# Two transformer blocks on one core: seven small loads on another queue, three modulation steps earlier, and a rewritten entry to the second block

## The chip, the cores and the metric

The kernel runs on one core of a Trainium2 chip. The metric is the device time of one execution in microseconds (us); below, "the profiled execution" is a separate one that was recorded instruction by instruction. TensorE is the matrix engine, VectorE (DVE in the rows) and ScalarE (ACT) do elementwise work, GpSimd (POOL) and SyncE (SP) here mostly issue DMAs.

## The reference

A sequence of 256 tokens with 1024 features passes through two layers of a first block and one layer of a second one, all in float32. What matters here:

```
# first block, layer 0 (attention) and 1 (pooling), 6 modulation vectors per layer
m = silu(c) @ w_mod[i] + b_mod[i]            # 1024 -> 6 x 1024, one row
hx, hc = x*(1+sc1)+sh1, ctx*(1+csc1)+csh1
q, k, v = projections of hx and hc by w_qkv; q, k of hx rotated by cos/sin tables
y = differential attention(q, [k_ctx,k], [v_ctx,v], lam(attn_lambda)) -> rms * subln_g -> w_o
x = layer_norm(ALPHA*x + g1*y, ln_g, ln_b)
x = layer_norm(ALPHA*x + g2*(silu(h@Wg)*(h@Wu))@w_out, ln_g, ln_b)   # h = x*(1+sc2)+sh2
# second block
h = rms(x, norm1_g);  columns of h @ w_in: a_q a_k a_v i_q i_k i_w b_q b_kv b_g c_qkv gates
a: an index score (i_q, i_k, i_w) picks the top 64 keys per query, attention over these
b: compressed, selected and window attention;  c: dilated attention
x = x + (sum over a,b,c of sigmoid(gate) * branch) @ w_out;  then a gated FFN
```

## The kernel before, in words

Every large product is exact to float32 in three passes: an operand is split in a high part (rounded to the matmul's float32r format) and a low part (the rest), and `mm3` (lines 77 to 80) issues high by high, high by low and low by high. Weights come in units of 1 MB: `raw_load` (line 54) takes one of four "raw" buffers and loads it by SyncE; `wsplit` casts each half on ScalarE (line 70) and subtracts on VectorE (line 71) into one of two to four split slots. A raw buffer is free again when both halves are split, a split slot when its last product is done.

The framework orders each engine's instructions ahead of time, by program order and its own estimate of when each is ready; then each engine runs its list strictly in that order, waiting where an operand is missing. `behind(i)` forces the instructions in its scope that run on i's engine to stand after i on it. `mod_step` (line 210) gives its instructions a lower priority.

*Modulation.* Ten vectors of 1024 (called sh2, sc2, g1 and so on) are made by 80 small steps. A step loads 512 KB of `w_mod` by POOL into one of three `mraw` buffers (line 131) and accumulates it on VectorE (line 132). Steps are strung into other stages: 2 behind each of 16 attention scores, 3 behind each of the pairs 2 to 10 of the first FFN (`STEPS_IN`), 1 behind each of the 11 units of its output product (`STEPS_OUT`), then, at `mod_until("g1_1")`, what is left of the vector g1 of layer 1. The finished row is broadcast by TensorE (line 145), and the last products of the first FFN stand behind that (`mods["mm"]`). The same three buffers also hold the layer norms' rows.

*Attention's entry.* Inputs and weights come in four quarters (`load_quarter`, SyncE); after the fourth, `rest(3)` finishes the products of quarter 3. Then, behind the last modulate activation on ScalarE (`seq["mod"]`), ScalarE issues seven small loads: five into `prow` (norm gains and biases, which one TensorE transpose, line 648, turns into columns), `rope` (256 KB, cos and sin tables) and `lamr` (128 KB, the lambda vectors). `rope_T` (lines 676 to 691) multiplies the projections by the tables on VectorE (lines 684 to 687) and transposes them on TensorE (line 690) for the scores.

*An FFN* (`Ffn`): its first two pairs of weight units are multiplied token tile by token tile (`tile_products`), so that they can begin when the first tile is normed; the other nine in `rest`; `out` multiplies by the output weights, in which the last `held` units are kept for `finish(t, n)`, tile by tile.

*Entry of the second block.* The second FFN's `out` is followed, for each token tile t, by `pre` (add the residual), `layer_norm`, `rms` and `to_hT` (8 transposes on TensorE, line 320, scaling on ScalarE, line 333, split on VectorE, lines 336 and 337). Then the buffers of the first block are given back; KZ (the zero-padded keys) is cleared by POOL; `small` and `pr2` are loaded by POOL, and `pr2` (key gains and positions) is transposed (line 956). `project(512, 452)` makes PA (a_k, a_v, the index vectors); its first weight unit is split under the last products of the FFN, the second while tile 0 is normed. The index vectors are transposed and put into place (lines 1150 to 1161), then `normed_dup_T` norms a_k (`kn`), then come the index scores, the top 64 and `project(0, 512)` (the queries a_q). `gates(0)` follows the attention in program order but fills TensorE during it.

`keep_busy(n)` (line 98) issues n products of a tile of ones, whose result nobody reads.

Of the kernel before, what the change touches and what calls it, by code (L numbers as in the profile page):

```python
# [10 lines left out]
F32 = mybir.dt.float32  # L11
# [20 lines left out]
def tile_net(ctx: ExitStack, tc: tile.TileContext, I: dict, out: bass.AP):  # L32
# [315 lines left out]
    class Out:  # L348
# [7 lines left out]
        def part(self, u, wh, wl, t, n):  # L356
            mh, ml = self.mov
            tk = slice(t * 128, (t + 1) * 128)
            for k in range(2):
                kk = 2 * u + k  # L360
                mm3(self.P[t][n], mh[:, kk, tk], ml[:, kk, tk], wh[:, k, HALF[n]], wl[:, k, HALF[n]], kk == 0,
                    kk == 2 * self.nu - 1)
# [16 lines left out]
    class Ffn:  # L379
# [16 lines left out]

        def tile_products(self, t, hT):
            hh, hl = hT
            tk = slice(t * 128, (t + 1) * 128)
            for fp in range(self.FIRST):  # L400
# [69 lines left out]
    with tc.tile_pool(name="at", bufs=1, side="right", reuse_waits="tile") as at:  # L470
# [48 lines left out]
        def load_quarter(q):  # L519

            raws = [raw_load(wv0[:, :, j0 * 128:(j0 + 2) * 128], 8, 256) for j0 in (8 + 2 * q, 2 * q)]
            load_x("x", q)
            rw = wp.tile([128, 2048], F32, tag="raw", name="raw", bufs=4)
            rw = rw[:, :1536].rearrange("p (w k c) -> p w k c", w=3, k=2)
            for i, kind in enumerate((1, 0, 2)):
                sp.dma_start(rw[:, i], wq[:, 2 * q:2 * q + 2, kind * 1024:kind * 1024 + 256])
                if i == 1:
                    load_x("ctx", q)
            return raws, rw
# [41 lines left out]
        class Chunk:  # L571
# [19 lines left out]
            def products(self, ks, lat=True, con=True):  # L591
# [7 lines left out]
                if self.kind and con:  # L599
                    if self.PC is None:  # L600
                        self.PC = bank().rearrange("p (t c) -> p t c", t=2)
                    for t in range(2):
                        tk = slice(t * 128, (t + 1) * 128)
                        for k in ks:
                            if self.kind == 1:
                                mm3(self.PC[:, t, :], wh[:, k, tk], wl[:, k, tk], hc[0][:, k, :], hc[1][:, k, :],
                                    k == 0 and t == 0, k == 7, **kw)
                            else:
                                mm3(self.PC[:, t, :], hc[0][:, k, tk], hc[1][:, k, tk], wh[:, k, :], wl[:, k, :],
                                    k == 0 and t == 0, k == 7, **kw)  # L610

# [4 lines left out]
        def rest(q):  # L616
            ks = range(2 * q, 2 * q + 2)
            cv.products(ks, con=False)
            ck.products(ks, lat=False)

        for q in range(4):
            with behind(*((first_dma.ins,) if not q else ())):
                raws, rw = load_quarter(q)
            mod_quarter(q, raws)
            if not q:
# [12 lines left out]

        with behind(seq["mod"]):
            prow = cp.tile([128, 128], F32, name="prow")  # L640
            gp.memset(prow, 0.0)
            se.dma_start(prow[32:64], I["ln_g"].rearrange("l w (k c) -> (l w k) c", c=128))
            se.dma_start(prow[64:96], I["ln_b"].rearrange("l w (k c) -> (l w k) c", c=128))
            se.dma_start(prow[96:104], rows128(I["norm1_g_2"][0]))
            se.dma_start(prow[104:112], rows128(I["norm2_g_2"][0]))
            se.dma_start(prow[112:113], I["attn_subln_g"])
            pcol_ps = sbank()
# [6 lines left out]
            N1, N2 = pcol[:, 96:104], pcol[:, 104:112]  # L654
            rope = at.tile([128, 2, 2, 2, 64], F32, name="rope")
            se.dma_start(rope, I["k_rope"].rearrange("(t p) v w c -> p t v w c", p=128))
            lamr = at.tile([128, 256], F32, tag="aT", name="lamr", bufs=5)
            se.dma_start(lamr, I["attn_lambda"].rearrange("a b c -> a (b c)").to_broadcast([128, 256]))

# [230 lines left out]
    with tc.tile_pool(name="hid", bufs=1, side="right", reuse_waits="tile") as hidp:  # L890
# [17 lines left out]
        for t in range(2):  # L908
# [4 lines left out]
            n4.rms(t)  # L913
            n4.to_hT(t, hT, N1)
            if t == 0:
                with behind(n4.scaled[0]):
                    n4.pre(1, 1, o3.finish(1, 1), grow)

# [4 lines left out]
    blk1.close()  # L923
    wi = kview(I["w_in_2"][0])
# [3 lines left out]
    seq["w"] = 2  # L928
    extras.append(ctx.enter_context(tc.tile_pool(name="wz", bufs=1, side="right", reuse_waits="tile")))
    with tc.tile_pool(name="b2", bufs=1, reuse_waits="tile") as b2:  # L930

        KZ = b2.tile([128, 6, 2, 2, 256], F32R, name="KZ")
        for half in range(2):
            gp.memset(KZ[(1 - half) * 64:(2 - half) * 64, :, :, half, :].bitcast(F32), 0.0)

# [7 lines left out]
        small = b2.tile([128, 554], F32, name="small")  # L945
        gp.dma_start(small, I["k_small"])
        cmask, eo, bmask = small[:, 0:256], small[:, 256:384], small[:, 384:392]
        nmask = small[:, 392:426].rearrange("p (t n) -> p t n", t=2)
        sel32 = small[0:32, 426:554]
        pr2 = b2.tile([128, 128], F32, tag="t512", name="pr2", bufs=3)  # L950
        gp.memset(pr2, 0.0)
        gp.dma_start(pr2[0:32], I["nsa_cmp_pos_2"][0].rearrange("s (l a) d -> (s l) (a d)", a=2))
        for dup in range(2):
            gp.dma_start(pr2[32:38, dup * 64:(dup + 1) * 64], I["qk_norm_g_2"][0])
        b = tbank()
        pe.transpose(b[:, :128], pr2, ident)
        pc2 = b2.tile([128, 41], F32, name="pc2")
        ve.tensor_copy(pc2[:, 0:38], b[:, 0:38])
        ve.tensor_mul(pc2[:, 38:41], b[:, 32:38:2], pc2[:, 33:38:2])
        GA, GB, GC = pc2[:, 38:39], pc2[:, 39:40], pc2[:, 40:41]  # L960
# [45 lines left out]
        def put(hi, lo, src, scale):  # L1006

            se.activation(hi, src, AF.Copy, scale=scale)
            ve.scalar_tensor_tensor(lo, src, scale, hi.bitcast(F32), op0=ALU.mult, op1=ALU.subtract)

        def put_k(src, t, d0, scale=1.0):

            n, tk = src.shape[1], slice(t * 128, (t + 1) * 128)
            for half in range(2):
                p = slice(half * 64, (half + 1) * 64)
                put(KZ[p, d0:d0 + n, 0, half, tk], KZ[p, d0:d0 + n, 1, half, tk], src[p],
                    scale if isinstance(scale, float) else scale[p])

# [85 lines left out]

        def gates(br):
            g = b2.tile([128, 8, 256], F32, tag="gate", name="gate", bufs=1)
            for u in range(4):
                wh, wl = wunit(wi[:, :, 4572 + br * 1024 + u * 256:4572 + br * 1024 + (u + 1) * 256], 8, 256)
                G = bank().rearrange("p (a b) -> p a b", a=2)
# [35 lines left out]
        WA = [wtile(0, sp), wtile(4, sp)]  # L1145
        PA = project(512, 452)
        vA = b2.tile([128, 2, 64], F32, name="vA")
        iwc = b2.tile([128, 2, 4], F32, name="iwc")
        iqT = b2.tile([128, 2, 2, 256], F32R, tag="vv", name="iqT", bufs=1)
        for t in range(2):  # L1150
            se.copy(vA[:, t, :], PA[t][:, 64:128])
# [8 lines left out]
            put_q(iqT, bv[:, 0:2], t, 0)  # L1160
            put_k(bv[:, 2:3], t, 0)
        normed_dup_T(PA, 0, 1, 1, GA)
        madd = []
# [23 lines left out]
        for t in range(2):  # L1187
# [15 lines left out]
            split_oT(oA, 4, oTh, oTl, t)  # L1203
        gA_ = gates(0)
        P1 = project(1476, 384)
# [252 lines left out]
```

## Time and profile before

| | us |
|---|---|
| median of 3 runs | 1160.46 (1156.91, 1160.46, 1160.65) |
| the profiled execution | 1157.81 |
| its span, from first to last instruction | 1156.0 |
| TensorE busy in it | 1129.1 |
| VectorE busy | 829.0 |
| ScalarE busy | 575.8 |

[...] Times are from the span's start. A row's bracket is the idle time of the engine before it and what ended that. A busy TensorE is not TensorE at its peak, since products overlap and their ends are modelled.

### The profile page before, as it was taken

The page shows a single profiled execution, that of the slowest core. Times are in us where ns is not written, and L with a number is a line of the kernel's source. Part 1 is how long each engine was busy: PE and PEld are TensorE (multiplying, and loading weights), DVE is VectorE, ACT ScalarE, POOL GpSimd, SP SyncE. Part 2 cuts the span into 40 slices and gives each one's busy share as a digit, 9 for nine tenths or more (in the row PEclk, how much of TensorE's full clock was granted, in tenths as well). Part 3 has the DMA queues.
Part 4 walks back from the last instruction along what each step waited for, and adds up shares of the span by engine and source line. Part 5 has one row for each costly group of instructions (what it writes and reads, how often), then busy time and mean ns, then how long its engine had stood idle before and what let it go on. Part 6 is the DMA issues. An engine that isn't in the chain of part 4 may idle for free. (4 is left out here: it accounts for less than half of the span.)

```text
span 1156.0 us, 19870 instructions
## 1 busy us (share of the span) xinstructions
PE 1129.1 (98%) x7967; PEld 1035.3 (90%) x7967; DVE 829.0 (72%) x1547; ACT 575.8 (50%) x1017; POOL 83.9 (7%) x154
## 2 busy tenths in 40 slices
PE   8989999999999999999999889999999999999998
PEld 7979988889999877999988779989999989999986
DVE  5677887887887877856654779788788674655541
ACT  5643444576444436654543655455346356545430
POOL 0101110100111111000000020000100000000000
PEclk9999999999999999999999999999999999999999
DMA  9956545648998993867565353660456254664530
GB/s 311 324 174 212 183 155 174 219 146 285 313 317 291 341 353 121 249 217 257 210 222 175 109 180 121 179 200 29 146 160 223 77 178 147 219 199 167 215 113 37
DMA packets 149098, 229.69 MB, mean 199 GB/s; under 512 B 5708, under 2 KB 121051, under 8 KB 149006
## 3 DMA queue, kind: packets, MB, share of 16 engines
q1 hardware_dynamic: 133440, 176.10, 46.6%
q0 software_dynamic: 14672, 50.63, 13.0%
q10 hardware_dynamic: 894, 1.69, 0.5%
q8 instruction: 63, 1.03, 0.4%
q14 instruction: 29, 0.24, 0.1%
HBM read 226.36 MB, written 2.04 MB: 198 GB/s over the span
## 5 line engine op out<-in xcount | busy, mean ns | idle before, releaser
L71 DVE TENSOR_TENSOR wlo<-raw,whi 128x1024 fp32r<-128x1024 f32 (+2 forms) x318 | 372.7, 1193 | 135.2 <-ACT whi L70 133.7
L70 ACT CAST whi<-raw 128x1024 fp32r<-128x1024 f32 (+2 forms) x318 | 316.3, 1028 | 229.6 <-PE mm L80 86.7
L78 PE MATMUL mm<-hTh,whi 128*128 128x256 f32 x1056 | 299.1, 283 | 0.0
L80 PE MATMUL mm<-hTh,wlo 128*128 128x256 f32 x1056 | 298.9, 283 | 0.0
L79 PE MATMUL mm<-hTl,whi 128*128 128x256 f32 x1056 | 298.3, 282 | 0.0
L79 PEld LDWEIGHTS mm<-hTl,whi 128*128 128x128 f32 x1056 | 199.4, 189 | 0.3
L78 PEld LDWEIGHTS mm<-hTh,whi 128*128 128x128 f32 x1056 | 199.3, 189 | 0.3
L80 PEld LDWEIGHTS mm<-hTh,wlo 128*128 128x128 f32 x1056 | 199.3, 189 | 0.1
L78 PE MATMUL mm<-whi,hTh 128*128 128x256 f32 (+4 forms) x592 | 185.5, 314 | 2.3 <-DVE hTh L336 1.8
L80 PE MATMUL mm<-whi,hTl 128*128 128x256 f32 (+4 forms) x592 | 184.8, 313 | 0.4 <-DVE hTl L337 0.4
L79 PE MATMUL mm<-wlo,hTh 128*128 128x256 f32 (+4 forms) x592 | 184.3, 312 | 0.6 <-DVE wlo L71 0.6
L78 PEld LDWEIGHTS mm<-whi,hTh 128*128 128x128 f32 x592 | 112.4, 190 | 9.0 <-DVE hTh L336 2.9
L79 PEld LDWEIGHTS mm<-wlo,hTh 128*128 128x128 f32 x592 | 112.3, 190 | 4.9 <-DVE wlo L71 1.0
L80 PEld LDWEIGHTS mm<-whi,hTl 128*128 128x128 f32 x592 | 111.9, 189 | 5.2 <-DVE hTl L337 1.0
L132 DVE SCALAR_TENSOR_TENSOR acc<-mraw,csil,acc 128x1024 f32<-128x1024 f32 x80 | 102.2, 1280 | 10.0 <-DMA mraw<-in_w_mod_dram 9.6
L78 PE MATMUL mm<-whi,hid 128*128 128x512 f32 x264 | 104.3, 395 | 0.0
L79 PE MATMUL mm<-wlo,hid 128*128 128x512 f32 x264 | 104.2, 395 | 0.0
L80 PE MATMUL mm<-whi,hid 128*128 128x512 f32 x264 | 103.7, 393 | 0.0
L131 POOL DMA_DIRECT2D mraw<-in_w_mod_dram x80 | 42.6, 533 | 367.8 <-DVE acc L132 269.8
L79 PEld LDWEIGHTS mm<-wlo,hid 128*128 128x128 f32 x264 | 49.6, 188 | 11.6 <-issue 1.0
L80 PEld LDWEIGHTS mm<-whi,hid 128*128 128x128 f32 x264 | 49.6, 188 | 11.5 <-issue 0.7
L78 PEld LDWEIGHTS mm<-whi,hid 128*128 128x128 f32 x264 | 49.6, 188 | 11.4 <-issue 0.7
(329 smaller groups left out, 1556.6 us busy)
## 6 DMA issues: line engine op xcount, KB each, us to landing
raw<-in_ffn_w_in_dram SPq DMA_DIRECT2D x44, 1024.0 KB, 7.1
mraw<-in_w_mod_dram POOLq DMA_DIRECT2D x80, 512.0 KB, 5.0
raw<-in_ffn_w_out_dram SPq DMA_DIRECT2D x22, 1024.0 KB, 4.9
raw<-in_w_ffn_in_dram SPq DMA_DIRECT2D x22, 1024.0 KB, 5.2
raw<-in_w_in_dram SPq DMA_DIRECT2D x16, 1024.0 KB, 5.5
raw<-in_w_ffn_out_dram SPq DMA_DIRECT2D x11, 1024.0 KB, 5.0
raw<-in_w_in_dram SPq DMA_DIRECT2D x14, 768.0 KB, 4.4
raw<-in_attn_w_qkv_dram SPq DMA_DIRECT2D x9, 1024.0 KB, 8.4
```

What stands on the lines that cost most here:

```text
L70: se.copy(hv[:, sl], raw[:, sl])
L71: seq["sub"] = ve.tensor_sub(lv[:, sl], raw[:, sl], hv[:, sl].bitcast(F32)).ins
L78: pe.matmul(o, lh, rh, start=first, stop=False, **kw)
L79: pe.matmul(o, lh, rl, start=False, stop=False, **kw)
L80: return pe.matmul(o, ll, rh, start=False, stop=last, **kw).ins
L131: gp.dma_start(raw, wv[:, k, g * 1024:(g + 1) * 1024])
L132: ve.scalar_tensor_tensor(acc, raw, csil[:, k, 0:1], acc, op0=ALU.mult, op1=ALU.add)
```

## The change

Three parts.

*Loads.* `load_quarter` keeps its last load as `seq["ld"]`; the seven small loads are issued by SyncE behind it, in quarter 3. What uses them (the transpose of `prow`, the lambda sums) stands behind the last product of `rest(3)` on TensorE, the last fill on ScalarE and VectorE.

*Modulation steps.* Each of the first FFN's two first pairs gets one step behind its last subtraction, a third stands behind the residual; the output product's last unit has none, and none is left for `mod_until("g1_1")`: before, that made two.

*Entry.* `pr2` is loaded and transposed before the second FFN's output product, in a buffer of the first block. Both weight units of PA are loaded and split behind the output product's units; the second one's split lies in two raw buffers. `finish(1, 1)` moves ahead of tile 0's transposes, six dummy products stand behind it, and these transposes stand behind the dummies. `small` is loaded before KZ is cleared. PA's products go tile by tile, with 14 dummies behind those of tile 0. `normed_dup_T` comes before the index vectors, and the casts and subtractions of the first gates' weights stand behind the last of the index keys' (`seq["ix"]`). The third split slot `wz` is used in another turn (`seq["w"]` is 0 instead of 2).

```diff
@@ tile_products(self, t, hT, mod_first=0)
-                    ve.tensor_sub(self.hid[1][:, fs, :], b, self.hid[0][:, fs, :].bitcast(F32))
+                    last = ve.tensor_sub(self.hid[1][:, fs, :], b, self.hid[0][:, fs, :].bitcast(F32)).ins
+                    with behind(last):
+                        mod_step(mod_first)
@@ out
-                    mod_step(mod_out)
+                    mod_step(mod_out if u < 10 else 0)
@@ quarters
+            if q == 3:
+                with behind(seq["ld"]):
+                    prow = cp.tile([128, 128], F32, name="prow")
+                    gp.memset(prow, 0.0)
+                    sp.dma_start(prow[32:64], I["ln_g"].rearrange("l w (k c) -> (l w k) c", c=128))
+                    sp.dma_start(prow[64:96], I["ln_b"].rearrange("l w (k c) -> (l w k) c", c=128))
...
+                    sp.dma_start(rope, I["k_rope"].rearrange("(t p) v w c -> p t v w c", p=128))
+                    lamr = at.tile([128, 256], F32, tag="aT", name="lamr", bufs=5)
+                    sp.dma_start(lamr, I["attn_lambda"].rearrange("a b c -> a (b c)").to_broadcast([128, 256]))
...
-        with behind(seq["mod"]):
-            prow = cp.tile([128, 128], F32, name="prow")
-            gp.memset(prow, 0.0)
-            se.dma_start(prow[32:64], I["ln_g"].rearrange("l w (k c) -> (l w k) c", c=128))
...
+        with behind(seq["mod"], seq["rest"], *seq["fill"]):
             pcol_ps = sbank()
             pe.transpose(pcol_ps[:, :128], prow, ident)
@@ first FFN
-            f.tile_products(t, hT)
+            f.tile_products(t, hT, 1)
...
+        with behind(*n1.mid):
+            mod_step()
@@ second FFN, entry of the second block
         f.rest(hT, 1, 3)
+        pr2 = pools["xp"].tile([128, 2, 128], F32, tag="f", name="pr2", bufs=4)[:, 0, :]
+        gp.memset(pr2, 0.0)
...
         o3 = f.out(I["ffn_w_out"][1], 3)
+        wi = kview(I["w_in_2"][0])
+        uA = [raw_load(wi[:, 4 * u:4 * u + 4, 512:964], 4, 452) for u in range(2)]
+        uA[0] = wsplit(uA[0], 4, 452, 0)
+        parts = [wp.tile([128, 2048], F32R, tag="raw", name=nm, bufs=4)[:, :1808].rearrange("p (a b) -> p a b", a=4)
+                 for nm in ("whi", "wlo")]
+        for sl in (slice(0, 2), slice(2, 4)):
+            se.copy(parts[0][:, sl], uA[1][:, sl])
+            ve.tensor_sub(parts[1][:, sl], uA[1][:, sl], parts[0][:, sl].bitcast(F32))
+        uA[1] = parts
...
             n4.rms(t)
-            n4.to_hT(t, hT, N1)
+            if t == 0:
+                P11 = o3.finish(1, 1)
+            with behind(*((keep_busy(6, o3.last),) if t == 0 else ())):
+                n4.to_hT(t, hT, N1)
...
-        PA = project(512, 452)
+        PA = [bank(), bank()]
+        for t in range(2):
+            tk = slice(t * 128, (t + 1) * 128)
+            for k in range(8):
+                wh, wl = uA[k // 4]
+                i = mm3(PA[t][:, :452], hT[0][:, k, tk], hT[1][:, k, tk], wh[:, k % 4, :], wl[:, k % 4, :], k == 0, k == 7)
+            if t == 0:
+                keep_busy(14, i)
...
+        normed_dup_T(PA, 0, 1, 1, GA)
...
-        normed_dup_T(PA, 0, 1, 1, GA)
...
-        gA_ = gates(0)
+        gA_ = gates(0, *seq["ix"])
```

## Rows read from the trace of the kernel before

**Rows 1.** The page: busy time of TensorE, and its clock in 40 slices.
```profile
PE 1129.1 (98%) x7967; PEld 1035.3 (90%) x7967; DVE 829.0 (72%) x1547; ACT 575.8 (50%) x1017; POOL 83.9 (7%) x154
...
PEclk9999999999999999999999999999999999999999
```

**Rows 2.** Busy time by stretches: length, then each engine, clock, DMA share, GB/s.
```profile
35.00:40.00 5.00, 5.00 (x44) 4.39 (x42) 3.06 (x6) 1.63 (x4) 0.00 (x0) 1.00 1.09 347
...
60.00:70.00 10.00, 7.45 (x52) 7.25 (x51) 7.26 (x20) 4.38 (x6) 0.00 (x0) 0.85 0.41 119
...
650.00:660.00 10.00, 8.12 (x33) 6.64 (x34) 6.38 (x22) 7.13 (x23) 0.00 (x0) 0.83 0.71 210
...
670.00:680.00 10.00, 6.85 (x37) 5.46 (x36) 4.97 (x14) 4.20 (x11) 2.58 (x5) 1.00 0.88 254
680.00:690.00 10.00, 8.19 (x60) 7.31 (x59) 9.85 (x37) 6.03 (x12) 0.00 (x0) 1.00 0.17 62
```

**Rows 3.** Waits of TensorE: total us, times, longest.
```profile
PE s L648 <- DMA prow<-in_norm_g_dram: 0.7, 1, 0.7
```

**Rows 4.** Timeline of the attention's entry: start, us, instruction, idle before it.
```profile
38.15 0.43 SPq L526 DMA_DIRECT2D raw<-in_attn_w_qkv_dram  x1
...
45.47 1.66 ACT L588 CAST whi<-raw 128x512 fp32r<-128x512 f32 x3
...
53.21 0.32 ACTq L642 DMA_DIRECT2D prow<-in_ln_g_dram  x1
...
61.78 0.69 DVE L684 TENSOR_TENSOR r<-mm,rope 128x512 f32<-128x512 f32 x1 [1.63 <-DMA rope<-in_k_rope_dram]
63.58 0.23 DVE L663 SCALAR_TENSOR_TENSOR ljunk<-lamr 128x64 f32<-128x64 f32 x1 [1.11 <-DMA lamr<-in_attn_lambda_dram]
...
65.94 0.65 PE L690 MATMUL tp<-idsel,r 128*128 128x128 f32 x4 [2.55 <-DVE r L687]
...
67.33 0.42 PE L78 MATMUL mm<-whi,hcT 128*128 128x256 f32 x1
```

**Rows 5.** Modulation steps (group of the page), and timeline at both places.
```profile
L132 DVE SCALAR_TENSOR_TENSOR acc<-mraw,csil,acc 128x1024 f32<-128x1024 f32 x80 | 102.2, 1280 | 10.0 <-DMA mraw<-in_w_mod_dram 9.6
...
276.91 2.36 DVE L71 TENSOR_TENSOR wlo<-raw,whi 128x1024 fp32r<-128x1024 f32 x2 [2.11 <-ACT whi L70]
...
425.87 1.96 PE L145 MATMUL s<-acc,ones 128*128 128x512 f32 x4 [0.17 <-issue]
```

**Rows 6.** Timeline: six dummies at the start, then the second block's entry.
```profile
16.35 1.60 PE L103 MATMUL s<-ones 128*128 128x128 f32 x12
...
645.67 1.78 ACT L70 CAST whi<-raw 128x904 fp32r<-128x904 f32 x2
...
648.62 1.27 PE L320 MATMUL tp<-idsel,z 128*128 128x128 f32 x8 [0.92 <-ACT z L303]
650.40 0.61 PE L78 MATMUL mm<-whi,hTh 128*128 128x452 f32 x1 [0.52 <-DVE hTh L336]
...
658.19 1.27 PE L320 MATMUL tp<-idsel,z 128*128 128x128 f32 x8 [1.05 <-ACT z L303]
659.89 0.47 PE L78 MATMUL mm<-whi,hTh 128*128 128x452 f32 x1 [0.43 <-DVE hTh L336]
...
662.48 5.39 POOL L936 MEMSET KZ<- 64x3072 f32 x2 [81.70 <-ACT whi L70]
...
664.69 2.71 SPq L54 DMA_DIRECT2D raw<-in_w_in_dram  x2
...
669.38 1.05 POOL L954 DMA_DIRECT2D pr<-in_qk_norm_g_dram  x2
...
671.88 1.23 DVE L71 TENSOR_TENSOR wlo<-raw,whi 128x1024 fp32r<-128x1024 f32 x1 [2.65 <-ACT whi L70]
...
675.73 0.30 PE L956 MATMUL tp<-idsel,pr 128*128 128x128 f32 x1 [3.15 <-DMA pr<-in_qk_norm_g_dram]
...
684.37 0.30 PE L1003 MATMUL tp<-idsel,kn 128*128 128x128 f32 x1 [1.81 <-DVE kn L1042]
...
694.55 1.22 DVE L71 TENSOR_TENSOR wlo<-raw,whi 128x1024 fp32r<-128x1024 f32 x1
```

More of the change, by code (lines that the diff above doesn't have):

```diff
@@ L360, in part @@
                 kk = 2 * u + k
-                mm3(self.P[t][n], mh[:, kk, tk], ml[:, kk, tk], wh[:, k, HALF[n]], wl[:, k, HALF[n]], kk == 0,
+                self.last = mm3(self.P[t][n], mh[:, kk, tk], ml[:, kk, tk], wh[:, k, HALF[n]], wl[:, k, HALF[n]], kk == 0,
                     kk == 2 * self.nu - 1)
@@ L618, in rest @@
             cv.products(ks, con=False)
-            ck.products(ks, lat=False)
+            seq["rest"] = ck.products(ks, lat=False)
         for q in range(4):
@@ L623, in tile_net @@
                 raws, rw = load_quarter(q)
+            if q == 3:
[4 more added lines that the diff above has]
+                    sp.dma_start(prow[64:96], I["ln_b"].rearrange("l w (k c) -> (l w k) c", c=128))
+                    sp.dma_start(prow[96:104], rows128(I["norm1_g_2"][0]))
+                    sp.dma_start(prow[104:112], rows128(I["norm2_g_2"][0]))
+                    sp.dma_start(prow[112:113], I["attn_subln_g"])
+                    rope = at.tile([128, 2, 2, 2, 64], F32, name="rope")
+                    sp.dma_start(rope, I["k_rope"].rearrange("(t p) v w c -> p t v w c", p=128))
+                    lamr = at.tile([128, 256], F32, tag="aT", name="lamr", bufs=5)
+                    sp.dma_start(lamr, I["attn_lambda"].rearrange("a b c -> a (b c)").to_broadcast([128, 256]))
             mod_quarter(q, raws)
@@ L654, in tile_net @@
             N1, N2 = pcol[:, 96:104], pcol[:, 104:112]
[L655 to L658, printed above, removed]
             lsum = at.tile([128, 4], F32, name="lsum")
@@ L898, in tile_net @@
         f.rest(hT, 1, 3)
-        o3 = f.out(I["ffn_w_out"][1], 3)
+        pr2 = pools["xp"].tile([128, 2, 128], F32, tag="f", name="pr2", bufs=4)[:, 0, :]
+        gp.memset(pr2, 0.0)
+        gp.dma_start(pr2[0:32], I["nsa_cmp_pos_2"][0].rearrange("s (l a) d -> (s l) (a d)", a=2))
+        for dup in range(2):
+            gp.dma_start(pr2[32:38, dup * 64:(dup + 1) * 64], I["qk_norm_g_2"][0])
+        b = tbank()
+        pe.transpose(b[:, :128], pr2, ident)
+        pc2 = cp.tile([128, 41], F32, name="pc2")
+        ve.tensor_copy(pc2[:, 0:38], b[:, 0:38])
+        ve.tensor_mul(pc2[:, 38:41], b[:, 32:38:2], pc2[:, 33:38:2])
+        o3 = f.out(I["ffn_w_out"][1], 3)
+        wi = kview(I["w_in_2"][0])
[7 more added lines that the diff above has]
+        uA[1] = parts
         mod_until("g2_1")
@@ L927, in tile_net @@
     yacc = yo.tile([128, 8, 256], F32, name="yacc")
-    seq["w"] = 2
+    seq["w"] = 0
     extras.append(ctx.enter_context(tc.tile_pool(name="wz", bufs=1, side="right", reuse_waits="tile")))
     with tc.tile_pool(name="b2", bufs=1, reuse_waits="tile") as b2:
-        KZ = b2.tile([128, 6, 2, 2, 256], F32R, name="KZ")
-        for half in range(2):
-            gp.memset(KZ[(1 - half) * 64:(2 - half) * 64, :, :, half, :].bitcast(F32), 0.0)
         def vtile():
@@ L946, in tile_net @@
         gp.dma_start(small, I["k_small"])
+        KZ = b2.tile([128, 6, 2, 2, 256], F32R, name="KZ")
+        for half in range(2):
+            gp.memset(KZ[(1 - half) * 64:(2 - half) * 64, :, :, half, :].bitcast(F32), 0.0)
         cmask, eo, bmask = small[:, 0:256], small[:, 256:384], small[:, 384:392]
@@ L949, in tile_net @@
         sel32 = small[0:32, 426:554]
[L950 to L959, printed above, removed]
         GA, GB, GC = pc2[:, 38:39], pc2[:, 39:40], pc2[:, 40:41]
@@ L1006, in put @@
         def put(hi, lo, src, scale):
[L1008 to L1009 removed]
+            i = se.activation(hi, src, AF.Copy, scale=scale)
+            return i.ins, ve.scalar_tensor_tensor(lo, src, scale, hi.bitcast(F32), op0=ALU.mult, op1=ALU.subtract).ins
         def put_k(src, t, d0, scale=1.0):
@@ L1015, in put_k @@
                 p = slice(half * 64, (half + 1) * 64)
-                put(KZ[p, d0:d0 + n, 0, half, tk], KZ[p, d0:d0 + n, 1, half, tk], src[p],
-                    scale if isinstance(scale, float) else scale[p])
+                i = put(KZ[p, d0:d0 + n, 0, half, tk], KZ[p, d0:d0 + n, 1, half, tk], src[p],
+                        scale if isinstance(scale, float) else scale[p])
+            return i
         def put_q(dst, src, t, d0, scale=1.0):
@@ L1103, in split_oT, with gates @@
             ve.tensor_sub(oTl[:, :nb, tk], bv, oTh[:, :nb, tk].bitcast(F32))
-        def gates(br):
+        def gates(br, *after):
             g = b2.tile([128, 8, 256], F32, tag="gate", name="gate", bufs=1)
             for u in range(4):
-                wh, wl = wunit(wi[:, :, 4572 + br * 1024 + u * 256:4572 + br * 1024 + (u + 1) * 256], 8, 256)
+                with behind(*after):
+                    wh, wl = wunit(wi[:, :, 4572 + br * 1024 + u * 256:4572 + br * 1024 + (u + 1) * 256], 8, 256)
                 G = bank().rearrange("p (a b) -> p a b", a=2)
```

20 lines of the change are left out of this document (8 added, 12 removed).

## The prediction

> **What bounds the kernel now.** I read the page first. [...] Second I read the busy time by stretches of 10 us [rows 2]: the stretches that the change touches are among the worst. From 60 to 70 us TensorE is idle for 2.55 us and its mean clock is 0.85; from 650 to 660 it is idle 1.88 us at 0.83; from 670 to 680 idle 3.15 us at full clock; from 680 to 690 idle 1.81 us. Third, the waits and the timeline, to see which operand ends each of these.
>
> In the attention's entry [rows 3, 4] the parameters' loads are issued by ScalarE from 53.21 us on, behind its last modulate. TensorE waits 0.7 us for `prow`; `rope` lands when VectorE starts its product at 61.78 us, `lamr` when it starts the lambda sums at 63.58 us, and these sums stand in VectorE's order between the two halves of the rotation. So the rotated keys are ready only at 65.94 us, after 2.55 us of idle TensorE; then it runs at half clock (a 256-column product takes 0.42 us at 67.33 us).
>
> In the second block's entry [rows 6] TensorE waits for ScalarE's `z` at 648.62 (0.92 us) and 658.19 us (1.05), for the split `hT` behind each (0.52 and 0.43), then 3.15 us for the landing of `pr2`, whose loads POOL issues at 669.38 us because its KZ memset of 5.39 us, begun at 662.48, stands before them; and 1.81 us at 684.37 for `kn`, which VectorE makes late because the index work comes first.
>
> **The change part by part.** The sum is made against the profiled execution: 1157.81 us, span 1156.0.
>
> *Loads on SyncE.* The seven loads go behind the last load of quarter 3 (SyncE's queue issues it at 38.15 us) [rows 4]. They add seven issues there: 0.43 us each by that row, 3.0 us, in front of the next weights' load, which the first attention group's cast uses only near 58 us; 1.2 us of extra bytes stand in the same place (0.42 MB at the 347 GB/s of the stretch from 35 to 40 us [rows 2]). Both are hidden by that distance of some 19 us; without it the price would be at most these 4.2 us. The memset of `prow` has no operand, and POOL has nothing queued before it but the opening memsets. When do they land? The quarter's own last weights are cast at 45.47 us [rows 4], so the loads behind them land at about 46 to 48 us, 10 us before the first use. Then `prow` costs nothing (0.7 us gained) and the rotation starts when its product ends near 57 us instead of at 61.78. What is late next: VectorE's own chain, 0.69 + 0.41 + 0.42 + 0.68 = 2.2 us, to about 59.5 us, while TensorE has 60 products of the contexts (0.117 us apart, 7 us) to do from 57.2. So the 2.55 us go, and with them the half clock: (1 - 0.85) x 10 = 1.5 us of full-clock work [rows 2]. Sum 0.7 + 2.5 + 1.5 = 4.7; bounds 0 (the rotation stays late) and 5.2; I take 4.5.
>
> *Three modulation steps into the first pairs.* A step is 1.28 us of VectorE and a 512 KB load [rows 5]. At their new place, 265 to 277 us, VectorE idles 0.69 + 0.36 + 0.47 + 2.11 us (the last in [rows 5]), and the splits run ahead of TensorE by about half a weight unit or more (2.8 us of TensorE), so the 3.84 us are covered; uncovered they would cost 3.84. The loads wait for the same three buffers as the residual's rows, which come free at 259.5 and 260.7 us; a third is loaded already. At their old place, the end of the first FFN, TensorE loses 0.17 us before the row's products at 425.87 us, and VectorE stands 3.07 us for the last load, but what waits behind it are splits that TensorE does not need before 457 us. Bounds -3.8 and +0.5; I take +0.2, nearest to the 0.17.
>
> *Second block's entry.* (a) The first unit pair's casts leave the norm chain: today two casts (1.78 us from 645.67) and their subtractions stand in front of the scale and delay the first `z` by 0.94 us (the root's input is ready at 646.41, the root starts at 647.35). They move under the preceding FFN's output products, where ScalarE idles 3.4 us per unit. (b) Six dummy products, which the transposes must wait for: by the row at 16.35 us [rows 6] six take 1.60 us. From the last product (its end about 647.55) that gives transposes at 649.1 instead of 648.62 and, with the 1.78 us from transposes to first product of today, products at about 650.9 instead of 650.40: 0.5 lost. (c) If the clock then stays full, (1 - 0.83) x 10 = 1.7 us come back. (d) Fourteen dummies behind tile 0: 3.7 us by the same row, but only in so far as they don't fit the wait for tile 1 (1.05 + 1.27 of transposes + 0.43). Tile 1's residual sum may start some 1.2 us earlier (its product is finished first, and VectorE has no splits), so I let the second product start 1.0 us earlier: net gain of (a) to (d) 1.0 us, bounds -1.7 (all 28 dummy instructions in the way) and +2.2. (e) The `pr2` wait goes with its cause: +3.15 us. Its loads now stand behind the modulation's, some 50 us before use. (f) `kn` first: +1.81 us; next late would be the first gate weights. They are the price: two raw buffers hold the second unit's split until the last product of the pair (about 664), so the gates' loads, issued today at 664.69 and earlier, all come then and land some 5.5 us later, near 670; and their casts stand behind the index keys' split. TensorE has the 48 query products (0.233 us apart, 11.2 us), transposes and index scores to do meanwhile, until about 679. Bounds for (e) and (f): 0 and 5.2; I take 4.5, since VectorE, idle 2.65 us before 671.88 and about 3 us after it today [rows 6], has room there.
>
> The whole: 4.5 + 0.2 + 1.0 + 4.5 = 10.2 us, so 1147.6 us beside the profiled execution. The median of the runs is 2.65 us above that execution, and the runs reach from 1156.91 to 1160.65; I count from the middle of median and profiled run, 1159.1, and forecast **1149 us**.
>
> **Where clock and trace are weighed.** An idle time of 3.15 us before 675.73 us left the clock at 1.00, while 2.55 us before 65.94 and some 1.4 us around 648.62 were followed by half clock [rows 2, 4, 6]. The same idle time thus doesn't always cost. [...]
>
> **Rivals.**
> 1. *VectorE holds the second block.* From 680 to 710 us it is busy 9.9 of each 10 us (the first 10 us stand in [rows 2]); if its order keeps the mask's late end, TensorE only waits elsewhere and (e), (f) are lost. For it: that load. Against: its idle time from 668 to 676 is caused by the same `pr2` wait. 1159.1 - 5.7 = 1153.4.
> 2. *The loads don't do it*: the rotation waits for something else. Against: the two landings stand right before VectorE's starts [rows 4]. 1159.1 - 5.7 = 1153.4.
> 3. *The clock falls again* at the two places or at new ones: 3.2 us less, 1152.
> 4. *The gates come late, slower*: the planned order puts all eight half splits behind the index chain. TensorE eats a half unit in 2.8 us (24 x 0.117); today four halves stand 3.25 us apart in VectorE's order (from 684.79 to 694.55 [rows 6]). At 4.7 us apart eight would cost 8 x 1.9 = 15.2 us: 1164.1, slower than before; it decides from 4.7 us on. Against it: the first of them can start near 672.
> 5. *Little is left over*: a reordered plan gives back what it wins, 1157 to 1163.
>
> **How the numbers follow.** Forecast 0.55 (its own range 1144 to 1152), rival 1 0.15, rival 2 0.05, rival 3 0.10, rival 4 0.07, rival 5 0.08. About 0.3%, 3.5 us, is what a measurement can tell here: faster is below 1157.0, slower above 1163.9. Faster: the forecast and rivals 1 to 3, less 0.04 for their upper tails, 0.81; slower 0.07; within, 0.12. Range: from 1143 (all upper ends, 5.2 + 0.5 + 2.2 + 5.2 = 13.1, and the runs' spread) to 1158, which leaves the better part of rivals 4 and 5 out.
>
> **What would show it.** Right: no TensorE wait on `prow` or `pr2`; the first rotated transposes near 60 us and no half clock before 75 us; VectorE's three steps between 265 and 277 us with no wait for a weight split beside them; the first query product of the second block by about 664 minus what was won before, the first gate product some 5 us earlier relative to it. Wrong: TensorE waiting for gate weights' splits or their load after the query products, the twenty dummies standing in a row before tile 1's transposes with these already ready, or a gain at 65 us that is lost by 110 us to VectorE.

## The result and the profile after

The changed kernel takes 1150.29 us (median of its five executions) beside 1158.18 us for the kernel before: a ratio of 0.9929, 95% interval [0.9908, 0.995]. One of the five took 2827.72 us for a reason that no trace shows; the ratio leaves it out. A second set (e9 below) gives 1150.29 against 1157.76, 0.9942 [0.9929, 0.9956]. So by the two ratios it is 6.7 to 8.2 us faster, where 10.1 were forecast from a base of 1159.1; the time itself was forecast as 1149.

The profiled execution of after spans 1149.4 us. Its busy time and clock in the stretches that answer to [rows 2] (the columns: the stretch, then busy us and instructions of TensorE, its weight loads, VectorE, ScalarE and GpSimd, the granted clock, 1.00 being full, DMA share and GB/s):

```profile
60.00:70.00 10.00, 10.00 (x83) 9.46 (x82) 9.43 (x14) 8.09 (x11) 0.00 (x0) 1.00 0.73 249
650.00:660.00 10.00, 10.00 (x67) 9.39 (x65) 6.58 (x16) 8.66 (x20) 2.68 (x2) 1.00 0.18 52
670.00:680.00 10.00, 10.00 (x56) 8.22 (x55) 8.67 (x18) 9.28 (x17) 0.00 (x0) 1.00 0.94 283
680.00:690.00 10.00, 9.67 (x83) 9.47 (x82) 9.97 (x30) 5.11 (x7) 0.00 (x0) 1.00 0.55 185
```

All four stretches look cured: TensorE is busy and at full clock. In the second of them this is in part a false cure, since dummies count as busy.

**First attention group.** The timeline of after by engine (start us, duration, engine, line, operation, in brackets the idle time before it and what ended it), in answer to [rows 4]: SyncE's queue issues the parameters' loads from 39.96 us on, VectorE does the lambda sums at 54.94 and starts the rotation at 56.86, and TensorE has the rotated keys at 60.42 with no idle time.

```profile
39.96 0.41 SPq L632 DMA_DIRECT2D prow<-in_ln_g_dram  x1
44.35 0.78 SPq L640 DMA_DIRECT2D lamr<-in_attn_lambda_dram  x1
54.94 0.23 DVE L669 SCALAR_TENSOR_TENSOR ljunk<-lamr 128x64 f32<-128x64 f32 x1
56.86 0.68 DVE L690 TENSOR_TENSOR r<-mm,rope 128x512 f32<-128x512 f32 x1
60.42 0.60 PE L696 MATMUL tp<-idsel,r 128*128 128x128 f32 x4
```

**Modulation steps.** VectorE does the three steps in the first FFN's first pairs; no idle time of TensorE stands beside them.

```profile
263.48 1.28 DVE L132 SCALAR_TENSOR_TENSOR acc<-mraw,csil,acc 128x1024 f32<-128x1024 f32 x1
267.88 1.27 DVE L132 SCALAR_TENSOR_TENSOR acc<-mraw,csil,acc 128x1024 f32<-128x1024 f32 x1
270.20 1.28 DVE L132 SCALAR_TENSOR_TENSOR acc<-mraw,csil,acc 128x1024 f32<-128x1024 f32 x1
```

**Second block's entry**, in answer to [rows 6]. TensorE from the second FFN's last output product (643.35) to the first product of tile 1 (656.43); a dummy is two instructions:

```profile
643.35 0.40 PE L80 MATMUL mm<-whi,hid 128*128 128x512 f32 x1
643.58 1.50 PE L103 MATMUL s<-ones 128*128 128x128 f32 x12
644.92 1.04 PE L320 MATMUL tp<-idsel,z 128*128 128x128 f32 x8
647.29 0.47 PE L78 MATMUL mm<-whi,hTh 128*128 128x452 f32 x1 [1.33 <-DVE hTh L336]
...
652.40 1.28 PE L103 MATMUL s<-ones 128*128 128x128 f32 x10
653.57 0.66 PE L320 MATMUL tp<-idsel,z 128*128 128x128 f32 x4
654.06 0.39 PE L103 MATMUL s<-ones 128*128 128x128 f32 x2
654.28 0.60 PE L320 MATMUL tp<-idsel,z 128*128 128x128 f32 x4
654.72 1.95 PE L103 MATMUL s<-ones 128*128 128x128 f32 x16
656.43 0.46 PE L78 MATMUL mm<-whi,hTh 128*128 128x452 f32 x1
```

and ScalarE in the same time, with tile 1's first square (645.55) before tile 0's eight scalings (646.27):

```profile
642.90 1.34 ACT L303 ACTIVATE z<-x,nc 128x512 f32<-128x512 f32 x2 [0.23 <-DVE nc L267]
645.55 0.72 ACT L261 ACTIVATE sq<-z,nc 128x512 f32<-128x512 f32 x1 [1.31 <-DVE nc L287]
646.27 2.16 ACT L333 ACTIVATE f<-tp,pcol 128x128 f32<-128x128 f32 x8
```

The reader is to see two things: sixteen dummy instructions, 1.95 us, stand behind the last transposes of tile 1, where before the split of `hT` took 0.43 us [rows 6]; and 1.33 us of idle time that the six dummies don't cover but come in front of.

Further on, the wait for `pr2` is gone. That for `kn` is 0.87 us instead of 1.81 [rows 6]. VectorE shows why some of it stays: three splits of query weights (658.85, 3.49 us) stand before the second sum of squares (662.25).

```profile
658.85 3.49 DVE L71 TENSOR_TENSOR wlo<-raw,whi 128x1024 fp32r<-128x1024 f32 x3
662.25 0.21 DVE L1015 TENSOR_REDUCE ss<-sq 128x1 f32<-128x64 f32 x1
...
665.98 0.33 PE L1023 MATMUL tp<-idsel,kn 128*128 128x128 f32 x1 [0.87 <-DVE kn L1063]
```

### The profile page after: what moved, and what is told of

Same layout as the page of the kernel before. It is cut to its first block, busy times and chain, and to the rows that moved or that the text cites. A ratio compares the mean times of both kernels' runs of the same rounds, so it can differ in the third digit from the quotient of the medians.

```text
span 1149.4 us, 19941 instructions
## 1 busy us (share of the span) xinstructions
PE 1131.6 (98%) x8007; PEld 1040.1 (90%) x8007; DVE 831.6 (72%) x1547; ACT 575.3 (50%) x1017; POOL 84.1 (7%) x154
## 4 chain that ended last, share of the span: by engine, by line
PE 90%; DVE 7%; ACT 2%; issue 1%; DMA 0%; SPq 0%; DVEq 0%; ACTq 0%
PE mm L80 25%; PE mm L78 25%; PE mm L79 25%; PE tp L1099 2%; DVE wlo L71 2%; PE s L1071 2%; PE s L712 2%; PE tp L736 1%; PE tp L1095 1%; PE s L138 1%; PE s L543 1%; PE tp L723 1%; PE s L542 1%; PE mm L890 1%; PE s L145 1%
```

## Experiments

Four measures are used throughout, each a difference of two start times in one trace, so that the start of the kernel drops out. *Attention*: first modulated product to last score. *Entry*: the start of the second FFN's last output product to that of the last 452-column product. *Behind it*: from there to the first gate product. *Tile 1*: the same start as the entry, to tile 1's transposes, and to its first product.

| kernel | attention | tile 1: transposes, first product | entry | behind it |
|---|---|---|---|---|
| before | 191.02 | 10.88, 12.58 | 17.44 | 19.67 |
| after | 185.94 | 10.22, 13.08 | 17.89 | 16.36 |
| e1 loads alone | 185.10 | 10.86, 12.78 | 18.40 | 20.39 |
| e2 steps alone | 191.01 | as before | 17.43 | 22.41 |
| e3 entry alone | 189.85 | as after | 17.88 | 16.72 |
| e4 no dummies | 185.92 | 9.89, 11.59 | 17.95 | 15.13 |
| e5 square | 185.94 | 11.80, 13.50 | 18.37 | 16.09 |
| e6 nine | 185.96 | 10.23, 11.97 | 16.81 | 16.47 |
| e7 no six, nine | 185.95 | 9.89, 11.59 | 16.50 | 16.05 |
| e8 square, nine | 185.92 | 11.79, 13.49 | 19.92 | 15.14 |
| e9 after again | 185.98 | as after | 17.88 | 16.35 |
| e10 nine again | 185.92 | 10.22, 11.96 | 16.84 | 16.40 |
| e11 nine, `kn` later | 185.94 | as e10 | 16.78 | 16.15 |
| e12 no six, nine, `kn` later | 185.94 | as e7 | 16.50 | 16.11 |

**e1 to e3: the three parts of the diff, each alone on the kernel before.** Their edits are the three parts of the diff.

> The kernel before with the loads' part alone (seven parameter loads on SyncE behind quarter 3's, their first uses behind the quarter's fills and products). Theory 'the parts add': the trace of after has the first rotated transposes 7.0 us earlier and the last score 5.1 us earlier, both counted from the first modulated product; so this kernel is 4.5 to 5.1 us faster than before, with no TensorE wait on prow and no half clock from 60 to 75 us. Rival 'the plan ripples': the gain of after comes from the order that all parts make together, and this one alone gives under 3 us, or gives the 7 us and loses them to VectorE before 130 us.

Measured: 1152.49 us against 1158.5, ratio 0.9947 [0.993, 0.9964]: 6.1 us faster. The attention's stretch is 5.9 us shorter, more than the 4.5 to 5.1 expected; TensorE waits for `prow` no more and has full clock (1.00) from 60 to 75 us. The rival (under 3 us) falls.

> The kernel before with the three modulation steps alone (two in the first pairs, one behind the residual, and none behind the first FFN's last output unit). Prediction: 0.2 us faster. Theory 'the parts add', from the two traces: from the last score to the last hid product before the pool mix after is 0.9 us better than before (3.64 against 4.58 us), of which 0.4 us are lost at the pairs and given back at the row's products; so 0.2 to 0.9 us faster, which can't be told from no change. Rival: the steps delay the splits of the first whole-width units, up to 3.8 us slower.

Measured: 1158.37, 0.9994 [0.9977, 1.001]. No change that can be told, and not 3.8 us slower.

> The kernel before with the second block's entry alone. Prediction: 5.5 us faster (1.0 for the casts, dummies and the clock, 4.5 for pr2 and kn). Theory 'the parts add', from the two traces: only 2.7 us faster (3.96 us ahead at the last hid product of the second FFN, 6.64 at the end): the pr2 and kn waits give 3.3, and the norm and first products lose 0.5 where 1.0 was to be won. Rival 'clock and start': the part alone gives the whole 5.5 us, and after lost the difference to where its clock fell in other stages.

Measured: 1155.81, 0.9974 [0.9962, 0.9987]: 3.0 us faster. In its profile the entry is 0.44 us longer than in before, and what comes behind it 2.95 us shorter. It holds its clock at the entry (1.00 from 650 to 660 us) as after does, and the rival (5.5 us) lies outside the interval. The three ratios together make 1 - 0.0053 - 0.0006 - 0.0026 = 0.9915, within after's first interval and below the second ([0.9929, 0.9956]); with some 0.003 of uncertainty of its own (an estimate from the three intervals) the sum fits both. That the parts add is shown no more closely than that.

The profile of e3 also bears on the loads. It has the old ones, and waits 3.1 us for the rotated keys where before waits 2.55; but here full clock (1.00) followed, and the attention took 1.17 us less than in before. TensorE of e3 (busy us, instructions, granted clock, DMA share, GB/s):

```profile
60.00:70.00 10.00, 6.94 (x59) 1.00 0.47 137
```

So a part of the 5.9 us is a half clock that follows the old loads in some profiles (before 0.85, e2 0.84 from 60 to 70 us) and not in another (e3).

The traces of before, e1 and e2 show what the old entry costs from one execution to the next. In before the wait for `pr2` was followed by full clock [rows 2]; in e1 and in e2, which have the same instructions there, it was followed by half clock (0.83 and 0.72 on average from 670 to 680 us). The same columns of e1 and then of e2, where the wait was 2.50 and 3.18 us:

```profile
670.00:680.00 10.00, 8.18 (x35) 0.83 0.45 128
```

```profile
670.00:680.00 10.00, 6.82 (x25) 0.72 0.89 257
```

So 'behind it' takes 19.67, 20.39 and 22.41 us with the old entry, 20.8 on average; the one profile that the prediction had was the cheapest of three.

**e4: after without any dummy.**

```
-            with behind(*((keep_busy(6, o3.last),) if t == 0 else ())):
+            if True:
                 n4.to_hT(t, hT, N1)
...
             if t == 0:
-                keep_busy(14, i)
+                pass
```

> The kernel after without the six and the fourteen dummy products of the second block's entry. Theory 'the dummies stand in the way': in after the transposes of tile 0 start 1.3 us behind operands that are ready, and the products of tile 1 start 1.0 to 1.1 us behind their first hT; without dummies both go, up to 2 us faster than after if the clock stays full, some 0.3 us faster if it falls to half for one stretch of 3.4 us (1.7 us). Rival 'the dummies hold the clock': the clock falls at one or two places and the kernel is 0.5 to 3 us slower than after. Rival 'it is the order of ScalarE': nothing changes at the transposes, since the eight scalings still stand behind tile 1's first square.

Measured: 1149.25, 0.9918 [0.9901, 0.9935]; after's interval overlaps it. In the profile the clock fell at the entry (650 to 660 us: 0.83), and the entry takes 17.95 us beside 17.89: in the entry the twenty dummies cost what the clock costs, so each of the first two theories has its part; but the kernel is not the 0.5 to 3 us slower that the second named. The third isn't tested here, because the framework's plan, with no dummies to place, put tile 0's scalings first, and the wait for `hTh` went from 1.33 to 0.50 us:

```profile
642.51 0.39 PE L80 MATMUL mm<-whi,hid 128*128 128x512 f32 x1
644.62 0.48 PE L78 MATMUL mm<-whi,hTh 128*128 128x452 f32 x1 [0.50 <-DVE hTh L336]
...
652.40 1.27 PE L320 MATMUL tp<-idsel,z 128*128 128x128 f32 x8 [2.50 <-ACT z L303]
654.10 0.74 PE L78 MATMUL mm<-whi,hTh 128*128 128x452 f32 x1 [0.43 <-DVE hTh L336]
```

Tile 0 is ready 1.8 us earlier than in after, and tile 1's transposes only 0.33 us: they wait 2.50 us for `z`, which VectorE and ScalarE make. Behind the entry e4 is 1.23 us shorter than after. Beside e7 below, whose transposes of tile 1 come at the same 9.89 us but whose clock stays full, e4's entry is 1.45 us longer and the stretch behind it 0.92 us shorter: e7 then waits 0.7 us for `kn`, which VectorE makes, and e4, with the same order of products there, doesn't. So at the first gate product only 0.5 us of this half clock are left.

**e5 and e8: tile 1's statistics behind tile 0's splits**, with fourteen and with nine dummies:

```
-            n4.layer_norm(t, rows)
+            with behind(*(n4.done[0, 3] if t else ())): n4.layer_norm(t, rows)
```

> The kernel after, with tile 1's LayerNorm statistics issued behind tile 0's last scaling and split in the second block's entry, so that ScalarE does the eight scalings before tile 1's first square. The measure is the stretch from the start of the second FFN's last output product to the start of the entry's last product: 17.44 us in before, 17.89 in after, 17.95 in after without dummies. Theory 'ScalarE's order costs it': the 1.33 us wait for hTh of tile 0 falls to the 0.50 us that it is without dummies, 0.8 us; but the fourteen dummies stand in one row before tile 1's transposes in this order (3.5 us), so the stretch is 17.1 to 17.9. Rival 'the six dummies alone cost it': the wait stays over 1 us.

> The kernel after with tile 1's statistics behind tile 0's splits and nine dummies in place of fourteen; the six stay. Theory: 0.8 us from ScalarE's order and 0.6 to 1.1 from the dummies: stretch 16.2 to 16.8 us; it is as good as the kernel without the six, since these (1.5 us) then cost only what the wait for z does not cover, some 0.9 us, which makes 16.9 at worst. Rival: the gains do not add, since tile 1's statistics are now late by as much as tile 0's products are early: 17.4 us.

Measured: e5 1151.38, 0.9928 [0.9915, 0.9941]; e8 1150.26, 0.992 [0.9907, 0.9933]. The wait for `hTh` falls to 0.61 us with the six dummies in place, so ScalarE's order did cause most of it; yet nothing is won: the entry takes 18.37 and 19.92 us, more than the 17.9 and 17.4 us that the expectations allowed at most (in e8 the clock fell as well, 0.83 from 650 to 660 us). In e8 tile 1's first square now starts at 647.84 us, behind the scalings, and tile 1's transposes come 1.6 us later than in after (11.79 against 10.22). ScalarE and TensorE of e8:

```profile
644.22 2.18 ACT L333 ACTIVATE f<-tp,pcol 128x128 f32<-128x128 f32 x8 [1.31 <-PE tp L320]
647.84 0.72 ACT L261 ACTIVATE sq<-z,nc 128x512 f32<-128x512 f32 x1 [1.45 <-DVE nc L287]
653.80 1.27 PE L320 MATMUL tp<-idsel,z 128*128 128x128 f32 x8 [1.27 <-ACT z L303]
```

So the early square, which is the fault behind the 1.33 us, buys tile 1's `z`; that is the chain that sets the end.

**e6 and e7: nine dummies for fourteen**, with the six and without:

```
-                keep_busy(14, i)
+                keep_busy(9, i)
```

> The kernel after with nine dummies in place of fourteen behind tile 0's products; nothing else. Theory 'the last eight dummies stand before ready products': three stand there now, 5 x 0.25 us less, of which 0.6 to 1.1 us are on the path: stretch from last output product to the entry's last product 16.8 to 17.3 us (after 17.89), clock full. Rival 'they hold the clock': it falls to half behind them and the stretch is 18.3 us or more.

> The kernel after without the six dummies and with nine in place of fourteen. Theory: tile 0's transposes start at once (1.0 us earlier than in after, as without dummies), tile 1's wait is filled, and the clock stays full: stretch 16.2 to 16.8 us, 1.1 to 1.7 us less than after, and up to 1.2 us more from the order of kn that the kernel without dummies also has; whole kernel 1147 to 1149 us by the same scale as after's 1150.3. Rival: the idle 0.5 us before tile 0's products, or what is left before tile 1's transposes, lets the clock fall: 17.9 us or more, no gain on after.

Measured: e6 1148.3, 0.9907 [0.9893, 0.9921], entry 16.81; e7 1148.5, 0.9908 [0.9894, 0.9922], entry 16.50. The theory holds in both: the clock stays full at the entry (1.00 from 650 to 660 us), and the 1.08 us that e6's entry wins are the dummies that stood in front of ready products. Without the six only 0.3 us more is won, since tile 1's transposes then wait 0.53 us for `z`; and of the up to 1.2 us expected from the order of `kn` 0.3 came (16.05 beside after's 16.36). It is no better in time than e6.

**e9 to e12, on one chip:** after as it is, nine dummies again, and `kn`'s transposes forced behind the 21st query product (e11 with the six, e12 without). In the traces they stand behind the 19th such product in e10 (not the second, as the expectation says) and behind the 24th in e11, so the move is a small one:

```
-                put_k(transposed(tmp, nh), t, d0, scale)
+                with behind(*after): put_k(transposed(tmp, nh), t, d0, scale)
...
-        normed_dup_T(PA, 0, 1, 1, GA)
+        PQ = project(0, 512, *n4.done[1, 1], units=(0,)); normed_dup_T(PA, 0, 1, 1, GA, seq["pj", 1, 2])
...
-        PQ = project(0, 512, *n4.done[1, 1])
+        project(0, 512, *n4.done[1, 1], units=(1,), PL=PQ)
```

> The kernel after as it is, for a comparison on one chip with the three that follow. Expected where its first runs lay, 8.2 us below before; its stretch from the second FFN's last output product to the entry's last product is 17.9 us again. Its profile shows also whether the half-clock stretches at 11 to 15 and 452 to 455 us belong to the kernel or to one execution.

> The kernel after with nine dummies in place of fourteen, once more beside after. Theory: 1.1 us of dummies that stood before ready products are gone, so 1.1 to 2 us faster than after on the same chip. Rival: its first runs, 2.2 us below after against kernels before on different chips, were scatter, and no difference remains.

> The kernel after with nine dummies, and kn's two transposes behind the 21st query product in TensorE's order instead of the second (4.9 us of products in front of them). Theory 'only the place in TensorE's order is wrong': the wait for kn (0.9 us in after, 1.2 us with nine dummies) goes, and from the entry's last product to the first gate product it is 15.1 to 15.4 us as in the kernel without dummies, 1 us less than with nine alone. Rival 'VectorE holds the stretch': the index scores are then some 2 us later, VectorE ends the mask later, and what is won here is lost again at the first attend or at query's norm: no difference from nine alone.

> The kernel after without the six dummies, with nine for fourteen and with kn's transposes behind the 21st query product. Theory: the gains add to those of the same kernel without the move (stretch to the entry's last product 16.5 us, then 16.05 us to the first gate product): 16.5 and 15.1 to 15.4, the fastest of all, about 3 us below after. Rival as for the kernel above: VectorE gives the 0.7 to 0.9 us back before the first branch product.

Measured: e9 1150.29 (0.9942 [0.9929, 0.9956]), e10 1147.65 (0.9917 [0.9903, 0.9932]), e11 1148.61 (0.9926 [0.9913, 0.9939]), e12 1148.97 (0.9928 [0.9915, 0.9942]). Nine dummies beat both kernels: the slowest run of e10 (1148.86) lies below the fastest of e9 (1149.05). Of that gain 1.04 us are in the entry; the last section shows that another 1.1 us lie in the second FFN, far from the dummies. TensorE of e10, with six dummy instructions where after has sixteen:

```profile
642.17 0.40 PE L80 MATMUL mm<-whi,hid 128*128 128x512 f32 x1
...
653.54 0.83 PE L103 MATMUL s<-ones 128*128 128x128 f32 x6
654.13 0.45 PE L78 MATMUL mm<-whi,hTh 128*128 128x452 f32 x1
...
664.93 0.33 PE L1023 MATMUL tp<-idsel,kn 128*128 128x128 f32 x1 [1.12 <-DVE kn L1063]
```

Moving `kn`'s transposes doesn't help; the rival holds, and e12, expected to be the fastest, is not. The wait for `kn` (1.12 us) goes, but from the entry's end to the first gate product only 0.25 us are won, where about 1 was expected. TensorE's waits from 655 to 726 us (what waited, for whom, total us, times, longest), first of e10 and then of e11, show where the rest stands now:

```profile
PE tp L1023 <- DVE kn L1063: 1.1, 1, 1.1
PE s L1071 <- DVE mx L1077: 0.6, 1, 0.6
PE mm L79 <- DVE oTl L1124: 0.2, 1, 0.2
```

```profile
PE mm L78 <- ACT oTh L1123: 0.7, 1, 0.7
PE tp L1188 <- DVE KZ L1029: 0.5, 1, 0.5
PE tp L1120 <- DVE oA L1230: 0.3, 1, 0.3
PE mm L79 <- DVE oTl L1124: 0.3, 1, 0.3
PE s L1071 <- DVE mx L1077: 0.2, 1, 0.2
```

The sum is 1.9 us in e10 and 2.0 in e11: the wait for `kn` is paid at the index keys' split (VectorE) and, behind the attention, at `oA` and its copies and splits (ScalarE and VectorE). From the first gate product to the attention branch's first output product e11 takes 49.46 us (673.77 to 723.23), e10 48.41 (675.41 to 723.82).

## Why the prediction was right, and where not

**Loads: right, and undersized.** 4.5 us were taken, 5.9 measured in the attention (e1) and 6.1 by the ratio, both above the prediction's own upper bound of 5.2 (the ratio's interval reaches down to 4.2). The steps stand: no wait on `prow`, rotated transposes at 60.42 us (predicted near 60), no half clock from 60 to 75 us (1.00; the one that after's profile has between 10 and 20 us, mean clock 0.83, lies ahead of the change and is missing in e9), and no product of the attention waits behind the seven issues. In after the attention wins 5.1, 0.8 less than in e1; the last section has a finding on that. That the 1.5 us of the half clock were there to be won was in part luck: e3 has the old loads and no half clock in this place (1.00 against before's 0.85, 60 to 70 us).

**Modulation steps: right**, nothing that can be told. The steps stand at 263 to 271 us (predicted 265 to 277), and no product waits beside them.

**Entry, (a) to (d): wrong, by 1.4 us.** Forecast +1.0; measured -0.45 (17.44 to 17.89), the same in e3 and e9. Two terms failed.

(c) "If the clock then stays full, (1 - 0.83) x 10 = 1.7 us come back." They don't. In e1, whose entry is that of before, tile 0's products ran at full clock and took 4.87 us instead of 6.37 (before's clock was 0.50 from 651.0 to 653.5 us), and tile 1's transposes came at 10.86 instead of 10.88 us: TensorE only waited longer for `z`, 2.55 us instead of 1.05.

```profile
641.68 0.39 PE L80 MATMUL mm<-whi,hid 128*128 128x512 f32 x1
652.54 1.73 PE L320 MATMUL tp<-idsel,z 128*128 128x128 f32 x8 [2.55 <-ACT z L303]
```

The half clock of before lay in time that VectorE and ScalarE owned. In e1 it then fell on tile 1's transposes (1.73 us instead of 1.27) and products, where less covers it, and the entry grew by 0.96 us; in e4 and e8 it fell on tile 1's products alone, and these took 6.4 us (11.59 to 17.95, 13.49 to 19.92) where they took 4.9 at full clock (e7, 11.59 to 16.50), 1.5 us more. So in these four traces, all with a mean clock of 0.83 from 650 to 660 us, the price of the half clock depended on what stood behind it: 0.02 us before tile 1's transposes in before, 1.5 us in e4 and e8. The 1.7 us of (c), worked out from that mean clock and the 10 us, is an estimate that holds alike for before, e1, e4 and e8; these rows come near it only in e4 and e8, whose products had nothing else to wait for.

(d) "Fourteen dummies ... only in so far as they don't fit the wait for tile 1." They were priced against the wait as a sum, but of their 28 instructions ten fitted the wait for `z`, two stood between the transposes, and sixteen behind them, where 0.43 us were to be filled. Tile 1's transposes did come 0.66 us earlier, but its first product, which was to start 1.0 us earlier, came 0.5 us later. e6 and e10 isolate it: five dummies less, 1.04 to 1.08 us. The prediction's own list had a near case, "the twenty dummies standing in a row before tile 1's transposes with these already ready", and counted it in the bound of -1.7, not in the value.

**(e) and (f), `pr2` and `kn`: the mechanism right, the size 1.2 us off by the profile.** 4.5 were taken, 19.67 - 16.36 = 3.3 measured; 0.87 us of waiting for `kn` and 0.2 for the index keys are left. The step that failed is "since VectorE ... has room there": it still does three query splits first. Of the two idle times of VectorE that the prediction put down to `pr2`, only the second (2.96 us) ended with its transpose; the first (2.65 us) ended with ScalarE's cast of a weight [rows 6]. e11 shows that another place of `kn`'s transposes in TensorE's order does not cure it. Against the average of the three profiles with the old entry (20.8) the gain is 4.5, because in two of them half clock followed the wait for `pr2` (mean 0.83 in e1, 0.72 in e2, from 670 to 680 us).

**The rivals.** Rival 1, VectorE, did not take the whole second block, but the waits that are left there mostly end with its results (e10's and e11's waits, 2 us in all). Rival 4: no product waited for a gate's weights. Rival 3, the clock: at the entry (650 to 660 us) it fell to a mean of 0.83 in all four profiles without dummies (before, e1, e2, e4), and of the ten with dummies in e8 alone (0.83; 1.00 in the other nine). What decides is not settled: e7 idles 0.5 + 0.5 + 0.43 us around tile 0's and tile 1's transposes and keeps full clock, e8 0.6 + 1.3 + 0.4 and doesn't, and each kernel here but two was profiled once.

**The total** came out near in part by luck: errors of both signs met, +0.6 to +1.4 us in the loads, -1.4 in the entry, -1.2 behind it, and a base 0.5 to 1.3 us too high. The gain itself, 6.7 to 8.2 us, is 1.9 to 3.4 us short of the 10.1 forecast.

## What to carry to other kernels

Before counting a stall or a half-clock stretch as a gain, ask which chain sets the next operand: if another engine makes it at the same time, TensorE's faster work turns into a longer wait (e1: 1.50 us less for tile 0's products, 1.50 more for `z`). Dummies that are to keep a clock up (here it stayed at 1.00 in nine of ten entries with them, in none of four without) belong only into time that is idle anyway, so place each against the wait it fills, one by one, and look at what stands ready behind the last of them: five too many cost 1.08 us in the entry (after against e6). An early instruction that delays one tile may be what brings the next in time (in e8 tile 1's transposes came 1.6 us later without it); move it only with both chains in view.

## What was not expected of the hardware

**A half clock that cost nothing, once more.** At the second FFN's start, e9 ran at full clock (1.00 from 450 to 460 us) and e10 at half for a part of these 10 us (mean 0.83), with the same instructions. e9 waited 0.73 us for `hTh` and 0.83 for a weight split; e10 0.38 and none above 0.1 us. TensorE by stretches, e9 and then e10:

```profile
450.00:460.00 10.00, 8.45 (x66) 1.00 0.96 256
```

```profile
450.00:460.00 10.00, 9.62 (x63) 0.83 0.96 278
```

and their timelines, the first FFN product, the weight split's and the first output product, e9 and then e10:

```profile
451.78 0.36 PE L78 MATMUL mm<-whi,hTh 128*128 128x256 f32 x1 [0.73 <-DVE hTh L336]
459.24 0.38 PE L79 MATMUL mm<-wlo,hTh 128*128 128x256 f32 x1 [0.83 <-DVE wlo L71]
580.64 0.48 PE L78 MATMUL mm<-whi,hid 128*128 128x512 f32 x1
```

```profile
452.95 0.55 PE L78 MATMUL mm<-whi,hTh 128*128 128x256 f32 x1 [0.38 <-DVE hTh L336]
460.40 0.39 PE L79 MATMUL mm<-wlo,hTh 128*128 128x256 f32 x1
580.68 0.48 PE L78 MATMUL mm<-whi,hid 128*128 128x512 f32 x1
```

From the first FFN product to the product at 459.24 and 460.40 they take 7.46 and 7.45 us. The kernel alone doesn't settle which execution has the half clock: after's first profile has it here (0.83), its second (e9) doesn't (1.00).

**One per cent in the pitch of the same products.** From there to the first output product (580.64, 580.68) e9 takes 121.40 us and e10 120.28, both at clock 1.00 and with TensorE busy throughout. TensorE's instructions up to there are the same, in the same order. Over the 864 products of the second FFN's nine whole pairs the mean distance from one start to the next is 119.3 ns in after, e4, e5, e7, e8 and e9, 118.0 in e3, e6, e10, e11 and e12, and 119.0 in before, e1 and e2. Both kernels that were profiled twice (after, nine) kept their value, so it seems to belong to the program; what sets it was not tried. It makes 1.1 of the 2.7 us by which e10's trace, counted from the first modulated product, is ahead of e9's; the other parts are 1.04 in the entry and 0.5 in the second block's first attention. The attention shows something like it: its 256-column products stand 117.8 to 118.1 ns apart in before, e1 and e2, and 119.6 to 119.7 in all the others. Over its some 700 such products that is about 1.2 us (an estimate), enough for the 0.8 us by which e1's attention is the shorter one. A part of a change that is worth less than this can't be read from one pair of profiles.
